# First two pairs of experts in TensorE's written order, and the branch for crowded experts moved behind the third pair's up products

## The chip, the cores and the metric

The kernel runs on one core of a Trainium2 chip. The metric is the time of one execution on the device, in microseconds (us), lower is better. A core has five engines that run side by side: TensorE (PE in the profile, with its weight loads as PEld), VectorE (DVE), ScalarE (ACT), GpSimd (POOL) and SyncE (SP). Here SP does no arithmetic: it issues the loads of all large weights. Engines wait for each other and for loads through semaphores.

## The reference, cut to what matters

Two blocks follow each other on 256 tokens of 1024 channels. The first has attention, a spatial gating unit and a mixture of experts; the second has convolutions, a linear recurrence and an MLP. The change lies in the mixture of experts, where every token goes to 2 of 32 experts:

```python
def hierarchical_moe(x, w_router_group, b_router_group, w_router_expert, b_router_expert,
                     w_gate, w_up, w_down):
    ...
    combine = (g_onehot[:, :, None] * (g_weight[:, None] * e_w)[:, None, :]).astype(x.dtype)
    out = jnp.zeros((n, D), dtype=x.dtype)
    for g in range(N_GROUPS):
        h = jax.nn.silu(jnp.einsum('nd,edf->nef', xt, w_gate[g])) * jnp.einsum('nd,edf->nef', xt, w_up[g])
        out = out + jnp.einsum('nef,efd->nd', h * combine[:, g, :, None], w_down[g])
    return out.reshape(B, S, D)
```

The kernel computes an expert only on the tokens that are routed to it, in 64 slots per expert.

## The kernel before, in words

**Pairs.** The 32 experts are taken as 16 pairs (`for i in range(16)`). A pair has 12 weight tiles of 1 MB (1,048,576 bytes) each: four of `w_gate`, four of `w_up`, four of `w_down`. For a pair, TensorE gathers the tokens of its slots into `xg` (L676, two halves of 16 matrix multiplies in the program, 32 passes in the trace for both), multiplies them with the gate tiles and the up tiles (L830), transposes the hidden activations `hs` into `hT` (L716), makes the slot tables of the next pair (`slots`, L692 and L697) and multiplies `hT` with the down tiles into `dn` (L964). ACT copies `dn` out as `y` (L722) and DVE makes its remainder (L723); later TensorE scatters `y` to the tokens (L729) and DVE adds it to `h` (L735). Between the up products and the transposes stands `act_mul`: ACT writes `silu(gate)` into `hs_hT` (L706) and DVE multiplies it with the up result (L707). DVE then copies the transposed tile (L717).

**Loads.** `Ring` holds the weight tiles in six pools (`ring_a` to `ring_f`, 5, 9, 2, 2, 1 and 2 buffers, 21 together). When a product has used up its tile, `ring.free` hands the buffer to the next tile in the list, and SP issues that load (L79) as soon as TensorE's last read of the buffer is over. SP issues in its own order, one load after the other. Each load counts on one of eight semaphores (`DMAHW0` to `DMAHW7`, in turn), and a load first waits for the one before it on the same semaphore, so at most eight are under way.

**Order.** From pair 2 on, `manual_schedule(engines={T.engine})` makes TensorE run in the order in which the code is written. For pairs 0 and 1 a scheduler orders TensorE's instructions.

**The branch.** An expert can have more than 64 tokens. `nmore` counts the blocks beyond; every engine reads it into a register `nb` (L943), and `overflow()` (branch at L841, loop at L868) works on these blocks if `nb > 0`. With the inputs of this case the loop isn't entered. In the loop SP loads weights into the buffer that `hidden()` gives, the same single buffer (tag `r4`) into which `hs_hT` and `y` of all pairs go:

```python
                w = hs_hT[:, 0].rearrange("p k c -> p (k c)")
...
                        nc.sync.dma_start(w, src[:, k // 2, k % 2])
```

In the kernel before, pair 1 ends with its whole scatter, and the branch stands between pair 1 and pair 2. After the last pair comes the second block, which begins with a normalisation of `h` and then multiplies with weights that come through `ring_a` alone (L1096).

Of the kernel before, what the change touches and what calls it, by code (L numbers as in the profile page):

```python
# [8 lines left out]
F32 = mybir.dt.float32  # L9
# [83 lines left out]
def kernel(ctx: ExitStack, tc: tile.TileContext, a: dict, out):  # L93
    nc = tc.nc
    V, S, T, G = nc.vector, nc.scalar, nc.tensor, nc.gpsimd
# [6 lines left out]
    ring = Ring(nc)  # L102
# [14 lines left out]
    W_EXP = []  # L117
# [50 lines left out]
    rows = p1m.tile([24, 128], F32, name="rows", tag="x41")  # L168
# [272 lines left out]
    ps = proj_ts(4)  # L441
# [290 lines left out]
    def scatter(gt, y, n, m):  # L732
        s = slice(512 * n, 512 * n + 512)
        for c in range(2):
            V.tensor_add(h[:, c, s], h[:, c, s], to_token(gt, c, m, y))  # L735

    def scatter_late(gt, y, dn, m):

        scatter(gt, y, 0, m)
        evac(dn, 1, m, y)  # L740
# [77 lines left out]
    nmore_i = mk.tile([128, 1], I32, name="nmore_i")  # L818
    V.tensor_copy(nmore_i, nmore)

    tile_done = []

    def products(i, n, ps, x, between=None):
        for q, idx in enumerate(W_EXP[i][n]):
            if q == 2 and between:
                between()
            t = ring.get(idx)
            for k in range(2):
                for j in range(2):
                    m = T.matmul(ps[64 * j:64 * j + 64, :], x[:, 2 * q + k, 64 * j:64 * j + 64], t[:, j, 512 * k:512 * k + 512],  # L830
                             start=q == 0 and k == 0, stop=q == 3 and k == 1, skip_group_check=True)
            ring.free(idx)
            if i == 0:
                tile_done.append(m)
                with tc.issue_after(m.ins):
                    for _ in range(2):
                        next(start, None)

    def overflow():

        with tc.If(nb > 0):  # L841
            nper = mk.tile([128, 32], F32, name="nper")
            V.tensor_add(nper, more[:, 0], more[:, 1])
            V.tensor_add(nper, nper, more[:, 2])
            pos = mk.tile([128, 3, 32], F32, name="pos")
            V.tensor_tensor_scan(pos[:, 0], ones[:, :32], nper, 0.0, op0=OP.mult, op1=OP.add)
            V.tensor_sub(pos[:, 0], pos[:, 0], nper)
            for m in (2, 1, 0):
                V.scalar_tensor_tensor(pos[:, m], pos[:, 0], float(m + 1), more[:, m], op0=OP.add, op1=OP.mult)
            V.tensor_scalar(pos, pos, -1.0, None, op0=OP.add)  # L850
            tabs = hidden()[:, 1].rearrange("p a (b c) -> p (a b) c", c=32).rearrange("p (m a) c -> p m a c", m=2)
            tab, sel = tabs[:, 0], tabs[:, 1]
            part = mk.tile([128, 8], F32, name="part")
            num = mk.tile([128, 32], F32, name="num")
            G.iota(num, pattern=[[1, 32]], base=0, channel_multiplier=0, allow_small_or_imprecise_dtypes=True)
            blocks = mk.tile([128, 2, 8], F32, name="blocks")
            V.memset(blocks, 0.0)
            for m in range(3):
                V.tensor_tensor(tab, iota[:, 0:8, None].to_broadcast([128, 8, 32]),
                                pos[:, m:m + 1, :].to_broadcast([128, 8, 32]), op=OP.is_equal)  # L860
                V.tensor_mul(sel, tab, num[:, None, :].to_broadcast([128, 8, 32]))
                V.tensor_reduce(part, sel, axis=AX.X, op=OP.add)
                V.tensor_add(blocks[:, 0], blocks[:, 0], part)
                V.tensor_reduce(part, tab, axis=AX.X, op=OP.add)
                V.scalar_tensor_tensor(blocks[:, 1], part, 64.0 * (m + 1), blocks[:, 1], op0=OP.mult, op1=OP.add)
            blocks_i = mk.tile([128, 8], I32, name="blocks_i")
            V.tensor_copy(blocks_i, blocks[:, 0])
            with tc.For_i(0, nb, 1) as b:  # L868
                ev = nc.sync.value_load(blocks_i[0:1, ds(b, 1)], min_val=0, max_val=31)
                evv = nc.vector.value_load(blocks_i[0:1, ds(b, 1)], min_val=0, max_val=31)  # L870
                cur = mw.tile([128, 7], F32, name="cur")
                V.tensor_copy(cur[:, 0:1], blocks[:, 1, ds(b, 1)])
                V.tensor_copy(cur[:, 1:3], rank[:, :, ds(evv, 1)].rearrange("t c o -> t (c o)"))
                V.tensor_scalar(cur[:, 1:3], cur[:, 1:3], cur[:, 0:1], None, op0=OP.subtract)
                V.tensor_copy(cur[:, 3:6:2], cwE[:, :, ds(evv, 1)].rearrange("t c o -> t (c o)"))
                V.tensor_copy(cur[:, 4:7:2], rf[:, :, 0])
                g = mw.tile([128, 2, 64], F32, name="g_ov", tag="onehot", bufs=1)
                V.tensor_tensor(g, iota[:, None, 1:65].to_broadcast([128, 2, 64]),
                                cur[:, 1:3, None].to_broadcast([128, 2, 64]), op=OP.is_equal)
                hs_hT = hidden()  # L880
                x = hs_hT[:, 1].rearrange("p a (b c) -> p (a b) c", c=64)
                for k0 in (0, 4):
                    gather_part(g, x, k0, 4)
                p = psM.tile([64, 2, 128], F32, name="ms")
                for c in range(2):
                    T.transpose(p[:, c], g[:, c], ident)
                gt = mk.tile([128, 2, 128], F32R, name="onehotT_ov")
                V.tensor_copy(gt[:64], p)
                p = psM.tile([64, 2], F32, name="ms")
                for c in range(2):  # L890
                    T.matmul(p, g[:, c], cur[:, 3 + 2 * c:5 + 2 * c], start=c == 0, stop=c == 1)
                cw = mk.tile([128, 2], F32, name="cw_ov")
                V.tensor_copy(cw[:64, 0:1], p[:, 1:2])
                V.tensor_mul(cw[:64, 1:2], p[:, 0:1], cw[:64, 0:1])
                ps = {}

                w = hs_hT[:, 0].rearrange("p k c -> p (k c)")
                for n in ("w_gate", "w_up"):
                    ps[n] = psE.tile([128, 512], F32, name="gate" if n == "w_gate" else "up")
                    src = flat[n][ds(ev, 1)].rearrange("o (q p k) f -> p (o q) k f", p=128, k=2)  # L900
                    for k in range(8):
                        nc.sync.dma_start(w, src[:, k // 2, k % 2])
                        T.matmul(ps[n][:64], x[:, k], w, start=k == 0, stop=k == 7)
                hT = transpose_h(act_mul(ps["w_gate"], ps["w_up"], cw, 64, hs_hT[:, 0]), 64, hs_hT[:, 1])
                dn = [psE.tile([128, 512], F32, name=f"dn{n}") for n in range(2)]
                src = flat["w_down"][ds(ev, 1)].rearrange("o (p k) f -> (o p) k f", k=4)
                for k in range(4):
                    for n in range(2):
                        nc.sync.dma_start(w, src[:, k, 512 * n:512 * n + 512])
                        T.matmul(dn[n][:64], hT[:, k, 0:64], w, start=k == 0, stop=k == 3)  # L910
                y = output()
                for n in range(2):
                    evac(dn, n, 64, y)
                    scatter(gt, y, n, 64)
# [8 lines left out]
    turn = ExitStack()  # L923
    steady = ExitStack()
    for i in range(16):
        if i == 2:


            steady.enter_context(tc.manual_schedule(engines={T.engine}))
        gate = psE.tile([128, 512], F32, name="gate")  # L930
        up = psE.tile([128, 512], F32, name="up")
        if i < 15:
            onehot(i + 1)
        products(i, "w_gate", gate, XG[i])
        if prev:
            scatter_late(*prev)
        if i == 0:
            with tc.issue_after(slots(0).ins):
                param_cols()
        with tc.issue_after(tile_done[0].ins) if i == 0 else ExitStack():  # L940
            products(i, "w_up", up, XG[i], (lambda: scatter(prev[0], prev[1], 1, 128)) if prev else None)
        if i == 0:
            nb = nc.values_load(nmore_i[0:1, 0:1], min_val=0, max_val=7)  # L943
        hs_hT = hidden()
        hs = act_mul(gate, up, CW[i], 128, hs_hT[:, 0])
        rows = gather(i + 1) if i < 15 else iter(())
        next(rows, None)
        if i < 2:
            next(rows, None)
            slots(i + 1)  # L950
        hT = transpose_h(hs, 128, hs_hT[:, 1])
        if 2 <= i < 15:
            next(rows, None)
            slots(i + 1)
        if i == 15:
# [14 lines left out]
        y = output()  # L970
        evac(dn, 0, 128, y)
        prev = (GT[i], y, dn, 128)
        if i == 1:
            scatter_late(*prev)
            scatter(GT[i], y, 1, 128)
            prev = None
            overflow()
    y2 = output("r2")
    evac(dn, 1, 128, y2)

# [537 lines left out]
```

## Time and profile before

| what | value |
|---|---|
| median of 3 runs (lowest to highest) | 1072.19 us (1071.92 to 1072.72) |
| the profiled execution's own time | 1072.1 us |
| its span, from the first to the last instruction | 1070.4 us |
| TensorE busy, share of the span | 1031.7 us, 96% |
| mean granted clock of TensorE | 0.985 of full speed |
| moved by DMA, mean rate | 299.70 MB, 280 GB/s |

The span is the time between the first and the last instruction of one profiled execution; 1.7 us of that execution's own time lie outside it. Busy shares are means over the whole span, and the stages have different limits, so the stretch from about 120 to 220 us, where the first three pairs run, is read by itself.

### The profile page before, as it was taken

To read this page: it belongs to the slowest core of one execution; us is meant where nothing else is said; L and a number is where in the kernel's file an instruction comes from. 1 tells how busy PE (TensorE), PEld (TensorE's weight loads), DVE (VectorE), ACT (ScalarE), POOL (GpSimd) and SP (SyncE) were. 2 spreads that over 40 slices of the span, in tenths; PEclk is the share of its full clock that TensorE was granted. 3 is DMA by queue.
4 is the path that set the end of the run, shared out by engine and by line. 5 is a ranking of instruction groups with operands and counts; after the bars stand their busy time and mean duration, and the time that the engine had idled before them with its cause. 6 is when DMAs were issued, how large, how long until landed. Compare 5 with 4: busy or idle time off the path is not lost.

```text
span 1070.4 us, 16246 instructions
## 1 busy us (share of the span) xinstructions
PE 1031.7 (96%) x6624; PEld 740.3 (69%) x6624; DVE 544.5 (51%) x1025; ACT 369.3 (34%) x596; POOL 221.4 (21%) x123
## 2 busy tenths in 40 slices
PE   8999998999999999999998899989897999999997
PEld 7998644444444444444444898869897999998996
DVE  4758433122222222222224889897986366555555
ACT  5565211000000000000002545866536445445443
POOL 0161000000000000000001887454885800000000
PEclk9999999999999999999999999989898999999999
DMA  9997899899999999999999664423462665655531
GB/s 315 301 358 278 311 368 410 339 409 409 408 409 410 409 409 409 409 408 409 409 409 368 190 196 160 133 88 117 158 197 95 193 206 185 205 181 180 195 117 40
DMA packets 138987, 299.70 MB, mean 280 GB/s; under 512 B 14325, under 2 KB 79325, under 8 KB 138909
## 3 DMA queue, kind: packets, MB, share of 16 engines
q1 hardware_dynamic: 138397, 297.32, 75.8%
q8 instruction: 53, 0.87, 0.3%
q10 hardware_dynamic: 432, 1.05, 0.2%
q0 software_dynamic: 80, 0.26, 0.1%
q14 instruction: 25, 0.20, 0.1%
HBM read 297.56 MB, written 1.05 MB: 279 GB/s over the span
## 4 chain that ended last, share of the span: by engine, by line
PE 72%; DVE 5%; issue 2%; POOL 1%; ACT 1%; POOLq 0%; DVEq 0%; ACTq 0%
PE acc L1096 22%; PE up L830 9%; PE dn L964 9%; PE gate L830 9%; PE acc L1416 8%; PE ms L676 5%; PE ms L729 3%; PE acc L1389 2%; PE acc L1347 2%; DVE acc L1158 1%; POOL w_lo L229 1%; PE acc L1224 1%; PE ms L716 1%; DVE vb L1247 1%; PE acc L1220 1%
## 5 line engine op out<-in xcount | busy, mean ns | idle before, releaser
L229 POOL TENSOR_TENSOR w_lo<-ring_a,w_hi 128x1024 fp32r<-128x1024 f32 (+1 forms) x77 | 186.4, 2437 | 535.3 <-ACT w_hi L228 534.4
L228 ACT ACTIVATE w_hi<-ring_a 128x1024 fp32r<-128x1024 f32 (+1 forms) x169 | 169.1, 1004 | 131.6 <-PE acc L1096 39.1
L229 DVE TENSOR_TENSOR w_lo<-ring_a,w_hi 128x1024 fp32r<-128x1024 f32 (+1 forms) x92 | 101.7, 1108 | 71.1 <-ACT w_hi L228 71.1
L1096 PE MATMUL acc<-n_hi,w_hi 128*128 128x256 f32 x448 | 119.3, 293 | 7.3 <-DVE rg L1236 4.6
L1096 PE MATMUL acc<-n_hi,w_lo 128*128 128x256 f32 x448 | 118.0, 290 | 1.8 <-POOL w_lo L229 1.8
L1158 DVE SCALAR_TENSOR_TENSOR acc<-ub,pcol,acc 128x256 f32<-128x256 f32 x232 | 104.0, 481 | 5.5 <-issue 2.8
L735 DVE TENSOR_TENSOR h<-h,ms 128x512 f32<-128x512 f32 x60 | 38.5, 683 | 125.7 <-PE ms L729 125.7
L722 ACT ACTIVATE y<-dn 128x512 fp32r<-128x512 f32 x32 | 19.0, 597 | 227.1 <-PE dn L964 113.0
L1096 PEld LDWEIGHTS acc<-n_hi,w_hi 128*128 128x128 f32 x448 | 88.2, 197 | 10.4 <-ACT acc L1229 4.7
L1096 PEld LDWEIGHTS acc<-n_hi,w_lo 128*128 128x128 f32 x448 | 88.1, 197 | 2.1 <-POOL w_lo L229 2.1
L723 DVE TENSOR_TENSOR y<-dn,y 128x512 fp32r<-128x512 f32 x32 | 21.9, 687 | 119.6 <-ACT y L722 119.6
L1096 PE MATMUL acc<-n_lo,w_hi 128*128 128x256 f32 x448 | 82.5, 286 | 0.0
L676 PEld LDWEIGHTS ms<-onehot,x_moe 128*128 128x128 f32 x512 | 59.9, 192 | 14.8 <-issue 13.0
L1096 PEld LDWEIGHTS acc<-n_lo,w_hi 128*128 128x128 f32 x448 | 66.9, 194 | 0.0
L676 PE MATMUL ms<-onehot,x_moe 128*128 128x128 f32 x512 | 64.4, 279 | 0.8 <-DVE onehot L666 0.8
L1096 PE MATMUL acc<-x2h,w_hi 128*128 128x256 f32 x256 | 64.6, 280 | 0.0
L1096 PE MATMUL acc<-x2h,w_lo 128*128 128x256 f32 x256 | 64.5, 281 | 0.0
L964 PE MATMUL dn<-ring_b,hs_hT 128*64 128x512 f32 x240 | 57.0, 597 | 0.0
L1416 PE MATMUL acc<-w_hi,fh 128*128 128x512 f32 x128 | 50.1, 391 | 0.0
L1416 PE MATMUL acc<-w_lo,fh 128*128 128x512 f32 x128 | 49.9, 390 | 0.0
L1416 PE MATMUL acc<-w_hi,fl 128*128 128x512 f32 x128 | 49.5, 391 | 0.0
L1096 PEld LDWEIGHTS acc<-x2h,w_hi 128*128 128x128 f32 x256 | 48.3, 189 | 0.6
(368 smaller groups left out, 2017.1 us busy)
## 6 DMA issues: line engine op xcount, KB each, us to landing
ring_a<-in_w_in_dram SPq DMA_DIRECT2D x32, 1024.0 KB, 9.1
ring_a<-in_w_dram SPq DMA_DIRECT2D x32, 1024.0 KB, 5.5
ring_b<-in_w_down_dram SPq DMA_DIRECT2D x30, 1024.0 KB, 18.4
ring_b<-in_w_gate_dram SPq DMA_DIRECT2D x26, 1024.0 KB, 18.3
ring_b<-in_w_up_dram SPq DMA_DIRECT2D x25, 1024.0 KB, 18.3
ring_a<-in_w_gate_dram SPq DMA_DIRECT2D x18, 1024.0 KB, 14.5
ring_a<-in_w_up_dram SPq DMA_DIRECT2D x15, 1024.0 KB, 12.1
ring_a<-in_w_down_dram SPq DMA_DIRECT2D x14, 1024.0 KB, 18.6
```

The costliest lines, as they stand in the source:

```text
L228: S.activation(hi[:, s], src[:, s], AF.Copy)
L229: steps.append(lambda s=s: E.tensor_sub(lo[:, s], src[:, s], hi[:, s].bitcast(F32)))
L676: T.matmul(p[:, k], xp[c][:, 128 * (k0 + k):128 * (k0 + k + 1)], g[:, c], start=c == 0, stop=c == 1)
L723: V.tensor_sub(y[:m, 1], dn[n][:m], y[:m, 0].bitcast(F32))
L729: T.matmul(p, gt[:m, c], y[:m, k], start=k == 0, stop=k == 1)
L735: V.tensor_add(h[:, c, s], h[:, c, s], to_token(gt, c, m, y))
L830: m = T.matmul(ps[64 * j:64 * j + 64, :], x[:, 2 * q + k, 64 * j:64 * j + 64], t[:, j, 512 * k:512 * k + 512], start=q == 0 and k == 0, st ...
L964: m = T.matmul(dn[n][64 * j:64 * j + 64], hT[:, k, 64 * j:64 * j + 64], t[:, j, 512 * n:512 * n + 512], start=k == 0, stop=k == 3, skip_gr ...
L1096: T.matmul(ps[:, b, :], w[:, k, b * 128:(b + 1) * 128], xx[4 * half + k], start=half == 0 and b == 0 and k == 0 and w is wh and not low, s ...
L1158: V.scalar_tensor_tensor(ca[:, j] if k == 30 else s, ub[:, j, k:k + 256], conv_a_w[:, 8 * k + j:8 * k + j + 1], s, op0=OP.mult, op1=OP.add)
L1347: T.matmul(pb[b // 2][:, b % 2, :], w[:, kk, b * 128:(b + 1) * 128], xx[:, kt], start=kt == 0 and b % 2 == 0 and q == 0, stop=kt == 11 and ...
L1416: T.matmul(out_ps[c][n], f[:, half, 128 * c:128 * c + 128], w[:, 0, 512 * n:512 * n + 512], start=j == 0 and half == 0 and q == 0, stop=j ...
```

## The change: what it does

Three things are done. First, TensorE's written order begins at pair 0. In pair 0 each gate tile is followed by the up tile of the same number, and the gathers that are still missing are written between them; pair 1 is written as all later pairs are, with pair 0's scatter inside its products. Second, `overflow()` moves from the end of pair 1 to a place in pair 2, behind its up products and ahead of its `act_mul`; pair 1's scatter goes into pair 2's products, and the one-hot table of pair 3 is made behind the branch. Third, since `gate`, `up` and `dn` are in use at the new place, the code in the branch takes its PSUM tiles from the pool `psM` (`ms`).

```diff
-    tile_done = []
-
-    def products(i, n, ps, x, between=None):
-        for q, idx in enumerate(W_EXP[i][n]):
-            if q == 2 and between:
-                between()
-            t = ring.get(idx)
-            for k in range(2):
-                for j in range(2):
-                    m = T.matmul(ps[64 * j:64 * j + 64, :], x[:, 2 * q + k, 64 * j:64 * j + 64], t[:, j, 512 * k:512 * k + 512],
-                             start=q == 0 and k == 0, stop=q == 3 and k == 1, skip_group_check=True)
-            ring.free(idx)
-            if i == 0:
-                tile_done.append(m)
-                with tc.issue_after(m.ins):
-                    for _ in range(2):
-                        next(start, None)
+    def product(i, n, ps, q):
+
+        t = ring.get(W_EXP[i][n][q])
+        for k in range(2):
+            for j in range(2):
+                T.matmul(ps[64 * j:64 * j + 64, :], XG[i][:, 2 * q + k, 64 * j:64 * j + 64], t[:, j, 512 * k:512 * k + 512],
+                         start=q == 0 and k == 0, stop=q == 3 and k == 1, skip_group_check=True)
+        ring.free(W_EXP[i][n][q])
...
-                    ps[n] = psE.tile([128, 512], F32, name="gate" if n == "w_gate" else "up")
+                    ps[n] = psM.tile([128, 512], F32, name="ms")
...
-                dn = [psE.tile([128, 512], F32, name=f"dn{n}") for n in range(2)]
+                dn = [psM.tile([128, 512], F32, name="ms") for n in range(2)]
...
     for i in range(16):
-        if i == 2:
-
-
+
+
+        if i == 0:
             steady.enter_context(tc.manual_schedule(engines={T.engine}))
         gate = psE.tile([128, 512], F32, name="gate")
         up = psE.tile([128, 512], F32, name="up")
-        if i < 15:
+        if i < 15 and i != 2:
             onehot(i + 1)
-        products(i, "w_gate", gate, XG[i])
-        if prev:
+        if i == 0:
+            for q in range(4):
+                for n, ps in (("w_gate", gate), ("w_up", up)):
+                    product(i, n, ps, q)
+                    for _ in range(2):
+                        next(start, None)
+                if q == 2:
+                    with tc.issue_after(slots(0).ins):
+                        param_cols()
+        else:
+            for q in range(4):
+                product(i, "w_gate", gate, q)
             scatter_late(*prev)
-        if i == 0:
-            with tc.issue_after(slots(0).ins):
-                param_cols()
-        with tc.issue_after(tile_done[0].ins) if i == 0 else ExitStack():
-            products(i, "w_up", up, XG[i], (lambda: scatter(prev[0], prev[1], 1, 128)) if prev else None)
+            for q in range(4):
+                if q == 2:
+                    scatter(prev[0], prev[1], 1, 128)
+                product(i, "w_up", up, q)
+        if i == 2:
+            steady.close()
+            overflow()
+            onehot(3)
+            steady.enter_context(tc.manual_schedule(engines={T.engine}))
...
-        if i < 2:
-            next(rows, None)
-            slots(i + 1)
         hT = transpose_h(hs, 128, hs_hT[:, 1])
-        if 2 <= i < 15:
+        if i < 15:
             next(rows, None)
             slots(i + 1)
...
-        if i == 1:
-            scatter_late(*prev)
-            scatter(GT[i], y, 1, 128)
-            prev = None
-            overflow()
```

How instructions move on the engines shows best at three places. The rows are the programs' orders, engine by engine; a row has the line, the operation, the tile written and the tiles read.

The first place is TensorE around the branch. In the kernel before, the last down products of pair 1 (`dn`), its scatter (`ms<-y,onehotT`), the register read and the branch stand together:

```order
L964 MATMUL dn_2047<-ring_a,hs_hT 64x512 x2
L964 MATMUL dn_2048<-ring_a,hs_hT 64x512 x2
L729 MATMUL ms<-y,onehotT 128x512 x8
L943 TENSOR_LOAD nmore_i
L841 COMPARE_AND_BRANCH
```

In the changed kernel, from pair 1's last down products to the branch (its line is now L832, that of the products L826), there stand:

```order
L966 MATMUL dn_2050<-ring_b,hs_hT 64x512 x2
L826 MATMUL gate<-ring_a,xg 64x512 x4
L826 MATMUL gate<-ring_b,xg 64x512 x4
L826 MATMUL gate<-ring_a,xg 64x512 x8
L729 MATMUL ms<-y,onehotT 128x512 x4
L826 MATMUL up<-ring_b,xg 64x512 x8
L729 MATMUL ms<-y,onehotT 128x512 x4
L826 MATMUL up<-ring_c,xg 64x512 x8
L832 COMPARE_AND_BRANCH
```

So the gate and up products of pair 2 have moved ahead of the branch, and the scatter now stands among them; the register read stands much earlier, behind pair 0's products.

The second place is SP, ahead of the branch. In the kernel before, the last of the 24 loads that stand between the read of `nmore_i` and the branch are these, with the semaphores that each waits for:

```order
L79 DMA ring_f<-in_w_up_dram 128x2x1024 [waits DMAHW6_49,PE_49]
L79 DMA ring_f<-in_w_up_dram 128x2x1024 [waits DMAHW7_49,PE_49]
L79 DMA ring_a<-in_w_up_dram 128x2x1024 [waits DMAHW0_49,PE_49]
L79 DMA ring_a<-in_w_up_dram 128x2x1024 [waits DMAHW1_49,PE_49]
L79 DMA ring_a<-in_w_down_dram 128x2x1024 [waits DMAHW2_49,PE_49]
L841 COMPARE_AND_BRANCH
L868 COMPARE_AND_BRANCH
L868 UNCONDITIONAL_BRANCH [waits SP_sequencer_49,DMAHW0_49,DMAHW1_49,DMAHW2_49,DMAHW3_49,DMAHW4_49,DMAHW5_49,DMAHW6_49,DMAHW7_49]
```

In the changed kernel there are 30 loads between the same two instructions, and the last of them are:

```order
L79 DMA ring_a<-in_w_down_dram 128x2x1024 [waits DMAHW3_49,PE_49]
L79 DMA ring_b<-in_w_down_dram 128x2x1024 [waits DMAHW4_49,PE_49]
L79 DMA ring_a<-in_w_down_dram 128x2x1024 [waits DMAHW5_49,PE_49]
L79 DMA ring_a<-in_w_gate_dram 128x2x1024 [waits DMAHW6_49,PE_49]
L79 DMA ring_b<-in_w_gate_dram 128x2x1024 [waits DMAHW7_49,PE_49]
L79 DMA ring_b<-in_w_gate_dram 128x2x1024 [waits DMAHW0_49,PE_49]
L832 COMPARE_AND_BRANCH
L859 COMPARE_AND_BRANCH
L859 UNCONDITIONAL_BRANCH [waits SP_sequencer_49,DMAHW0_49,DMAHW1_49,DMAHW2_49,DMAHW3_49,DMAHW4_49,DMAHW5_49,DMAHW6_49,DMAHW7_49]
```

Six more loads have moved ahead of the branch, and the last one now counts on `DMAHW0` instead of `DMAHW2`. The row with nine semaphores is the side on which the loop is skipped: SP waits there for all eight load semaphores.

The third place is ACT behind the branch. Before, from the end of the branch to the next pair's `hs_hT`:

```order
L841 UNCONDITIONAL_BRANCH [waits Activation_49]
L706 ACTIVATE hs_hT<-gate,cw 128x512 [waits DVE_49,DMAHW2_49,PE_49,Activation_49]
L694 ACTIVATE onehotT<-ms 128x256 [waits PE_49]
L722 ACTIVATE y<-dn_2378 128x512 [waits DVE_49,PE_49]
L722 ACTIVATE y<-dn_2379 128x512 [waits DVE_49,PE_49]
L706 ACTIVATE hs_hT<-gate,cw 128x512 [waits DVE_49,PE_49]
```

In the changed kernel:

```order
L832 UNCONDITIONAL_BRANCH [waits Activation_49]
L706 ACTIVATE hs_hT<-gate,cw 128x512 [waits DVE_49,DMAHW0_49,PE_49,Activation_49]
L694 ACTIVATE onehotT<-ms 128x256 [waits PE_49]
L722 ACTIVATE y<-dn_2381 128x512 [waits DVE_49,PE_49]
L722 ACTIVATE y<-dn_2382 128x512 [waits DVE_49,PE_49]
L706 ACTIVATE hs_hT<-gate,cw 128x512 [waits DVE_49,PE_49]
```

On ACT the rows read alike: in both kernels the first `hs_hT` behind the branch, that of pair 2, waits for one load semaphore, and the later ones for none. What moved is the branch ahead of it, and with it the load that this semaphore counts.

## Rows read from the trace of the kernel before

**Rows 1.** The page, parts 1 and 2: whole span, 40 slices of it.
```profile
span 1070.4 us, 16246 instructions
...
PE 1031.7 (96%) x6624; PEld 740.3 (69%) x6624; DVE 544.5 (51%) x1025; ACT 369.3 (34%) x596; POOL 221.4 (21%) x123
...
GB/s 315 301 358 278 311 368 410 339 409 409 408 409 410 409 409 409 409 408 409 409 409 368 190 196 160 133 88 117 158 197 95 193 206 185 205 181 180 195 117 40
```

**Rows 2.** The chain that ended last: start us, us, what; pair 2 on.
```profile
188.64 8.78 PE gate L830 x32
...
216.08 6.87 PE gate L830 x32
...
227.66 1.13 PE ms L729 x4
...
232.37 1.98 PE ms L676 x16
234.79 1.79 PE ms L676 x16
237.14 7.02 PE dn L964 x32
244.16 6.87 PE gate L830 x32
...
572.54 7.04 PE dn L964 x32
...
593.22 66.41 PE acc L1096 x552
```

**Rows 3.** TensorE's timeline, pairs 0 and 1: start us, us, line, tiles, idle before.
```profile
122.96 1.94 PE L830 MATMUL gate<-ring_a,xg 128*64 128x512 f32 x8
...
176.30 1.94 PE L964 MATMUL dn<-ring_f,hs_hT 128*64 128x512 f32 x8 [0.78 <-DVE hs_hT L717]
...
184.08 2.16 PE L729 MATMUL ms<-y,onehotT 128*128 128x512 f32 x6 [0.70 <-ACT y L722]
187.29 0.74 PE L729 MATMUL ms<-y,onehotT 128*128 128x512 f32 x2 [1.05 <-DVE y L723]
```

**Rows 4.** SP: two loads (timeline), and the branch's own instructions (source line).
```profile
183.43 0.37 SPq L79 DMA_DIRECT2D ring_a<-in_w_down_dram  x1
...
L841 SPq EVENT_SEMAPHORE  x9: 17/17/17, 184.4 to 194.4; - x9
...
194.53 0.38 SPq L79 DMA_DIRECT2D ring_a<-in_w_down_dram  x1
```

**Rows 5.** ACT's timeline behind the branch, and DVE's L707 (tile hs_hT).
```profile
197.51 0.69 ACT L706 ACTIVATE hs_hT<-gate,cw 128x512 f32<-128x512 f32 x1 [12.06 <-PE gate L830]
...
L707 DVE SCALAR_TENSOR_TENSOR hs_hT<-up,cw,hs_hT x16: 744/749/753, 141.3 to 569.3; 128x512 f32<-128x512 f32 x16
```

**Rows 6.** Windows: busy time of each engine, PEclk, DMA share, GB/s.
```profile
147.00:156.00 9.00, 9.00 (x46) 3.23 (x42) 0.05 (x1) 0.00 (x0) 0.00 (x0) 1.00 0.91 324
156.00:191.00 35.00, 31.50 (x149) 14.64 (x147) 11.07 (x20) 3.46 (x6) 0.00 (x0) 0.97 1.03 410
...
191.00:193.00 2.00, 2.00 (x10) 0.79 (x8) 0.00 (x0) 0.00 (x0) 0.00 (x0) 0.66 0.32 119
193.00:195.00 2.00, 2.00 (x12) 0.80 (x10) 0.00 (x0) 0.00 (x0) 0.00 (x0) 1.00 0.03 8
```

**Rows 7.** Windows at TensorE's lower clock, and TensorE's wait ahead of one.
```profile
189.00:192.30 3.30, 3.30 (x10) 1.22 (x8) 0.54 (x2) 0.00 (x0) 0.00 (x0) 0.50 0.79 312
...
708.90 0.55 PE L1096 MATMUL acc<-n_hi,w_hi 128*128 128x256 f32 x1 [4.56 <-DVE rg L1236]
...
707.80:714.50 6.70, 5.60 (x26) 5.64 (x27) 6.13 (x16) 6.67 (x14) 1.55 (x1) 0.50 0.00 0
```

**Rows 8.** The last loads of the experts: SP's timeline; the page's part 6.
```profile
552.85 9.67 SPq L79 DMA_DIRECT2D ring_a<-in_w_down_dram  x4
...
ring_b<-in_w_down_dram SPq DMA_DIRECT2D x30, 1024.0 KB, 18.4
```

## The prediction

> **What bounds the kernel now.** I first read the page's busy shares and slices [rows 1]: TensorE is busy for 1031.7 of 1070.4 us, and from the seventh slice to the 22nd DMA moves some 409 GB/s. So in the experts two things are near full at once, and the question is which of them ends last. The chain that ended last answers it for the time from 188 us on: it is TensorE alone, without a gap, from pair 2's gate at 188.64 to the last down products at 572.54, and a pair takes 244.16 - 216.08 = 28.08 us [rows 2]. Every microsecond by which pair 3's gate starts earlier or later than 216.08 therefore reaches the end of the experts. Behind them stand a normalisation and then, from 593.22, the second block's products, on the chain too [rows 2]; I take the shift through to the end unchanged.
>
> Ahead of 216.08, TensorE's own timeline shows where pairs 0 and 1 lose time [rows 3]: 0.78 us ahead of pair 1's down products, 0.70 and 1.05 us in pair 1's scatter, which has no other work beside it; the branch follows, and pair 2's gate takes 8.78 us where pair 3's takes 6.87 [rows 2], at a granted clock of 0.50, TensorE's 1.2 GHz level [rows 7].
>
> SP's timeline is what I looked at longest [rows 4]. Its last load ahead of the branch is issued at 183.43, the next one at 194.53. The nine waits of the branch lie between: SP waits until every load is in the core before it goes on. The windows agree [rows 6]: DMA runs at 410 GB/s up to 191, moves 119 in the next 2 us and 8 in the 2 after. This drain costs TensorE nothing now, since pair 2's gate and up tiles have long landed and its products run beside it. The first instruction behind the branch that needs the drain is ACT's L706 of pair 2, which writes the buffer that the skipped loop would have loaded into; its order row waits for the semaphore of the last load ahead of the branch. It started at 197.51, after 12.06 us in which it waited for TensorE's gate products [rows 5], 3 us after the drain's end. The wait was there, and something else ended later.
>
> **The change, part by part.**
>
> *Written order in pairs 0 and 1.* Pair 0 has 13.74 us of gate and up products (2 x 6.87 [rows 2]), three quarters of a gather (0.75 x (1.98 + 1.79) = 2.8) and one set of slots (237.14 - 234.79 - 1.79 = 0.56): 17.1 us from the first gate product at 122.96 [rows 3] makes 140.1. A gather, the transposes (234.79 - 232.37 - 1.98 = 0.44), slots and down products follow: 1.98 + 0.44 + 1.79 + 0.56 + 7.02 = 11.8, so pair 1's gate starts at about 151.9, and with the read of `nmore`, some half a microsecond, 152.4. Pair 1 takes 28.08 and pair 2 up to the end of its up products 232.37 - 216.08 = 16.29 [rows 2]: 196.8. If nothing else stood there, pair 3's gate would start 11.8 later, at some 209 with the branch, 7 us earlier than now. That is the most that this part can give on TensorE.
>
> *The branch behind pair 2's up products.* Now the drain stands right ahead of pair 2's L706, and there is no gate and up time of 16 us behind the branch to cover it. SP issues 30 loads ahead of the branch instead of 24. From 156 to 191 the loads ran at 410 GB/s without a hole [rows 6], so they are limited by transfer, not by free buffers; TensorE frees a buffer in 1.72 us (6.87 / 4) and a load takes 1.0486 MB / 410 GB/s = 2.56. Six more loads then end 6 x 2.56 = 15.4 us later: 194.53 + 15.4 = 209.9. One hole ahead may close: from 147 to 156 DMA moved 324 instead of 410 GB/s, which is 9 x (1 - 324 / 410) = 1.9 us, while SP waited for buffers that pair 0's down products now free one after the other; but their first comes no sooner than about 147, so I take half, 0.9, and as bounds 0 and 1.9. The drain ends at 209.0 (208.0 to 209.9).
>
> ACT then writes `hs` (0.69 us) [rows 5], DVE multiplies (0.75), TensorE transposes (0.44), gathers the second half (1.79), makes slots (0.56) and multiplies with the down tiles (7.02). The sum is 11.25, with 0.1 for the hand-overs 11.35: pair 3's gate at 209.0 + 11.35 = 220.35. The gather's first half needs no `hs` and is done by about 199.5, so TensorE stands for some 11 us.
>
> *The clock after that stand.* After a wait of 4.56 us the granted clock was 0.50 from about 707.8 to 714.5, and TensorE had begun again at 708.90 [rows 7], so 5.6 us of work ran at 1.2 GHz; of that half is lost, 2.8 us. The shorter stop ahead of pair 2's gate cost 8.78 - 6.87 = 1.91 us [rows 2]. This stand is longer than both; I take 2.6 and as bounds 1.0 (transposes and gather wait on ACT and DVE anyway, so a part may be hidden) and 3.2. Pair 3's gate starts at 222.95, which is 6.9 us later than 216.08.
>
> *What I cost at nothing.* All that is saved ahead of L706 (the stops of 0.78, 0.70 and 1.05 us, the slow gate of pair 2, up to 7 us in sum) is covered by the stand of 11 us. If that cover were gone, it would count in full. The early read of `nmore` and the one-hot of pair 3, now behind the branch, also end within the stand. The PSUM tiles in the loop concern instructions that don't run. The last down tile now lies in `ring_b`, so one more load of the second block may start early; from the last down products to 593.22 the chain waits on the normalisation, not on a load, so I count no gain.
>
> *The sum.* 6.9 us on the profiled execution's 1072.1 gives 1079.0. The median of the runs is 1072.19, 0.1 above that execution, so the two can be taken as one.
>
> The Trainium skill, on the page "DMA: Bandwidth & Descriptors" (section "Latency and other measured facts"), gives a fixed cost of about 2 us for a DMA, most of it the round trip of the receipt. The trace has more here: 238 KB moved from 191 on, 0.6 us' worth, so bytes ended at about 191.6 and SP went on 2.9 us later. By the page's figure the drain would end 0.9 us earlier and the time would be 1078.1; the measured tail is in the 194.53 that the sum starts from, so the sum keeps it.
>
> **The rivals.** *Faster: L706 doesn't stand behind the drain.* If the semaphore were met early, or if the loads landed before TensorE ends pair 2's up products at 196.8, TensorE's 7 us would come through. They would then meet the loads: the last down tiles are issued up to 562.5 and take 18.4 us from issue to landing [rows 8], while TensorE uses them from 572.54 to 579.58 [rows 2], so there are only some 3 us between, and 1 us from the closed hole. That gives about 4 us, 1068. For it: in the kernel before the same wait was invisible. Against it: it was invisible by 3 us only, and 15 us of loads are added. It decides where the drain ends: before 197 it is faster.
>
> *No change: the drain only moves.* If the drain lasted as long from its last load as now (194.53 - 183.43 = 11.1 us), that load would be issued when half of the up products are done, 232.37 - 227.66 = 4.7 us before their end, at 192.1, and the drain would end at 203.2; with 11.35 and 1.9 for the clock pair 3's gate starts at 216.5, 0.4 later: 1072.5. For it: nothing sets the queue's depth in the code but eight semaphores. Against it: TensorE would have freed 30 buffers in that time while DMA, at 2.56 us each and without a hole, cannot have moved more than some 24 or 25 of them.
>
> *Slower by more.* Loads could be held up further by SP's order, or the lower clock could fall into the down products for longer; each is inside the range.
>
> **How the numbers follow.** A measurement of this kernel tells 0.2%, 2.1 us, from no change. The forecast, a drain on the path, has a chance of 0.86; no change 0.06; faster 0.08. Its own bounds are 208.0 + 11.35 + 1.0 = 220.35 (4.3 later, 1076.4) and 209.9 + 11.35 + 3.2 = 224.45 (8.4 later, 1080.5). The stretches at the lower clock in the second block lie at other places after a shift and may add or take one loss of up to 1.7 us, so I give 1075.0 to 1082.0, and leave both rivals out.
>
> **What would show it.** Right: SP's first load behind the branch near 209; ACT's L706 of pair 2 right behind it, with its idle time ended by SP or a load and not by TensorE; a gap of 10 to 12 us on TensorE ahead of pair 2's transposes; a clock of 0.50 behind it; pair 3's gate near 223; 28.08 us a pair afterwards, and no gaps of a microsecond in pairs 0 and 1. Wrong would be the prediction if L706 started right after the up products, near 197; if SP's loads stopped well before 205; or if pairs behind the stand ran in less than 28 us, so that time was made good.

## The result, and the profile after

The changed kernel is slower: a median of 1079.43 us (1077.42 to 1080.12, 4 runs) against 1072.06 us for the kernel before on the same chip, a ratio of 1.0072 with a 95% interval of 1.0058 to 1.0086. The forecast was 1079.0, in a range of 1075.0 to 1082.0. The execution shown here took 1080.1 us, with a span of 1078.4; TensorE's busy time is 1033.8 us against 1031.7 [rows 1], so of the 8.0 us between the two spans 5.9 are time in which TensorE stood, and 2.1 are longer work.

TensorE's timeline of the changed kernel (start us, us, line, tiles, in brackets the idle time before and what ended it) shows where:

```profile
124.32 1.94 PE L826 MATMUL gate<-ring_a,xg 128*64 128x512 f32 x8
...
142.78 2.05 PE L676 MATMUL ms<-onehot,x_moe 128*128 128x128 f32 x16
...
154.47 3.60 PE L826 MATMUL gate<-ring_d,xg 128*64 128x512 f32 x16
...
182.54 1.89 PE L826 MATMUL gate<-ring_a,xg 128*64 128x512 f32 x8
...
195.34 3.65 PE L826 MATMUL up<-ring_c,xg 128*64 128x512 f32 x16
199.70 2.02 PE L676 MATMUL ms<-onehot,x_moe 128*128 128x128 f32 x16 [0.71 <-DVE onehot L666]
211.69 1.12 PE L716 MATMUL ms<-ident,hs_hT 128*128 128x128 f32 x4 [9.96 <-DVE hs_hT L707]
212.59 3.62 PE L676 MATMUL ms<-onehot,x_moe 128*128 128x128 f32 x16
```

The stops of [rows 3] are gone: no row of pairs 0 and 1 has a bracket. In their place stands one of 9.96 us in pair 2. The bracket names DVE's L707, which itself follows ACT's L706. ACT's timeline and SP's, of the same kernel, lead on:

```profile
210.16 0.69 ACT L706 ACTIVATE hs_hT<-gate,cw 128x512 f32<-128x512 f32 x1 [19.06 <-SPq L832]
```

```profile
192.61 2.08 SPq L79 DMA_DIRECT2D ring_b<-in_w_gate_dram  x2
210.67 0.38 SPq L79 DMA_DIRECT2D ring_c<-in_w_gate_dram  x1
```

In [rows 5] the idle time ahead of L706 was ended by TensorE's gate products; now the bracket names SP's branch, L832. What L706 itself waits for, by its order row, is `DMAHW0`, the semaphore of the last load ahead of the branch, and it starts 0.51 us before SP issues again: both follow the landing of that load. SP's two last loads ahead of the branch begin at 192.61 (the second at 194.3, by the row's length) and its next one stands at 210.67; before, the pair was 183.43 and 194.53 [rows 4]. The windows over this stretch (the last three columns are granted clock, DMA share and GB/s) show the loads running to their end, the empty time behind them, and the clock:

```profile
147.00:156.00 9.00, 9.00 (x47) 3.46 (x47) 2.01 (x7) 0.98 (x2) 0.00 (x0) 1.00 0.97 349
156.00:191.00 35.00, 35.00 (x178) 15.17 (x176) 7.71 (x16) 2.76 (x5) 0.00 (x0) 1.00 1.02 408
191.00:205.00 14.00, 10.02 (x52) 4.46 (x48) 2.87 (x5) 0.10 (x1) 0.00 (x0) 1.00 1.03 408
207.40:209.00 1.60, 0.00 (x0) 0.00 (x0) 0.00 (x0) 0.00 (x0) 0.00 (x0) 0.50 0.60 241
209.00:211.00 2.00, 0.00 (x0) 0.00 (x0) 0.12 (x1) 0.69 (x1) 0.00 (x0) 0.50 0.03 12
211.70:216.00 4.30, 4.30 (x20) 4.30 (x21) 1.22 (x2) 0.00 (x0) 0.00 (x0) 0.50 0.94 345
```

The chain that ended last shows that the delay is kept to the end:

```profile
224.31 6.87 PE gate L826 x32
...
252.38 6.87 PE gate L826 x32
...
580.77 7.04 PE dn L966 x32
...
601.53 67.67 PE acc L1093 x552
```

A pair still takes 252.38 - 224.31 = 28.07 us, the last down products start 8.23 us later than in [rows 2] and the second block 8.31 later. From there to the end of the span both kernels take 477 us.

### The profile page after: what moved, and what is told of

It is laid out like the page before. It is cut to its first block, busy times and chain, and to the rows that moved or that the text cites. A ratio compares the mean times of both kernels' runs of the same rounds, so it can differ in the third digit from the quotient of the medians.

```text
span 1078.4 us, 16243 instructions
## 1 busy us (share of the span) xinstructions
PE 1033.8 (96%) x6624; PEld 741.8 (69%) x6624; DVE 544.9 (51%) x1025; ACT 369.3 (34%) x596; POOL 222.2 (21%) x123
## 4 chain that ended last, share of the span: by engine, by line
PE 69%; DVE 5%; issue 2%; POOL 2%; ACT 2%; DMA 0%; POOLq 0%; DVEq 0%; ACTq 0%
PE acc L1093 21%; PE dn L966 9%; PE up L826 9%; PE gate L826 8%; PE acc L1413 8%; PE ms L676 5%; PE ms L729 3%; PE acc L1386 2%; PE acc L1344 2%; POOL w_lo L229 2%; DVE acc L1155 1%; PE ms L716 1%; DVE vb L1244 1%; DVE part L1294 0%; PE acc L1221 0%
## 5 line engine op out<-in xcount | busy, mean ns | idle before, releaser
L826 PE MATMUL up<-ring_b,xg 128*64 128x512 f32 x216 | 51.1, 597 | 0.0
```

The costliest lines, as they stand in the source:

```text
L826: T.matmul(ps[64 * j:64 * j + 64, :], XG[i][:, 2 * q + k, 64 * j:64 * j + 64], t[:, j, 512 * k:512 * k + 512], start=q == 0 and k == 0, st ...
```

## The experiments

All nine ran against the kernel before on the same chip as they did; the ratios are to that kernel. Its medians there were 1070.79 us for e1 to e4, 1071.96 for e5 to e9 and 1071.49 for e10, while the expectations start from 1072.1, or from 1079.4 for the changed kernel. So it is the ratios that are to be compared with them: e1's 1066.83 us is 0.9968 of its kernel before, 1068.7 on the scale of the expectations.

| run | what differs | median us | ratio, 95% interval |
|---|---|---|---|
| the change | | 1079.43 | 1.0072 (1.0058 to 1.0086) |
| e1_no_branch | changed kernel without the branch | 1066.83 | 0.9968 (0.9954 to 0.9982) |
| e2_own_buffer | changed kernel, the loop's loads into a buffer of their own | 1071.22 | 1.0004 (0.9995 to 1.0013) |
| e3_pool_loads | changed kernel, the loop's loads issued by POOL | 1067.38 | 0.9969 (0.9957 to 0.9981) |
| e4_order_only | written order, branch behind pair 1 | 1070.71 | 0.9998 (0.9989 to 1.0007) |
| e5_move_only | old order, branch in pair 2 | 1078.60 | 1.0067 (1.0050 to 1.0084) |
| e6_pair1 | changed kernel, branch in pair 1 | 1076.63 | 1.0051 (1.0032 to 1.0069) |
| e8_pair6 | changed kernel, branch in pair 6 | 1090.21 | 1.0180 (1.0163 to 1.0197) |
| e9_keep_busy | changed kernel, work in TensorE's stand | 1076.30 | 1.0041 (1.0027 to 1.0055) |
| e10_before_pool | kernel before, the loop's loads issued by POOL | 1070.82 | 0.9995 (0.9986 to 1.0004) |

**Take the branch away, or only its waits (e1 to e3).** Without the branch:

```diff
         if i == 2:
             steady.close()
-            overflow()
             onehot(3)
```

> The changed kernel without the branch and its loop (the blocks of experts with more than 64 tokens are left out; with these inputs none runs). Theory A, the drain on the path and behind it the pace of the loads: TensorE's stand of 10 us ahead of pair 2's transposes is gone, and with it the low clock; TensorE alone would then end the last down products 13.7 us earlier than in the changed kernel, 5.5 earlier than before. But from 192.2 us on, where the 59th load landed, the loads come at the 2.57 us that they took in the kernel before (128 of them from 216.14 to 545.29), so the 208th, the last down tile, lands near 575.3, and the last products end near 577.1 instead of 579.6: 1069.6 us, 2.5 under the kernel before. Rival B, TensorE alone bounds the experts: 1066.6. Rival C, the written order itself costs the time: it stays near 1079.

The loop's loads into a small buffer (`w_ov`, filled four times as often with a quarter each), so that nothing in `hs_hT`'s buffer is written by a load:

```diff
-                w = hs_hT[:, 0].rearrange("p k c -> p (k c)")
+                w = mk.tile([128, 128], F32, name="w_ov")
...
-                        nc.sync.dma_start(w, src[:, k // 2, k % 2])
+                        for f in range(0, 512, 128):
+                            nc.sync.dma_start(w, src[:, k // 2, k % 2, f:f + 128])
```

> The changed kernel, but the loop loads its weights into a small buffer of its own and not into the one that hs_hT uses, so ACT's L706 behind the branch waits for no load. SP's nine waits stay. Theory A: L706 of pair 2 starts right behind the up products, near 199; SP's loads still stop until about 210, the loads of 2.57 us each then end near 578.2 instead of 578.7 in the kernel before, and the end of the experts is where it was before: 1072.5 us, from 1071 to 1074. Rival B, TensorE alone bounds the experts: 1066.6. Rival C, the branch's own instructions or the empty load queue stop TensorE, whatever buffer is written: stays near 1079.

The same loads issued by POOL:

```diff
-                ev = nc.sync.value_load(blocks_i[0:1, ds(b, 1)], min_val=0, max_val=31)
+                ev = nc.gpsimd.value_load(blocks_i[0:1, ds(b, 1)], min_val=0, max_val=31)
...
-                        nc.sync.dma_start(w, src[:, k // 2, k % 2])
+                        nc.gpsimd.dma_start(w, src[:, k // 2, k % 2])
```

> The changed kernel, but the loop's loads are issued by POOL, so that the skipped side of the branch has no waits on SP's load semaphores. Theory A: no drain, no stop of SP's loads, no stand of TensorE, and the time is that of the kernel without the branch: 1069.6 us (last loads near 575.3). Rival B, TensorE alone: 1066.6. Rival C, the branch itself costs: near 1079; between 1070 and 1073 if compare and branch cost TensorE a microsecond or two.

ACT's row of L706 in pair 2, in the kernel with the buffer of its own and then in the one with POOL's loads:

```profile
200.25 0.69 ACT L706 ACTIVATE hs_hT<-gate,cw 128x512 f32<-128x512 f32 x1 [10.54 <-PEq L832]
```

```profile
197.87 0.69 ACT L706 ACTIVATE hs_hT<-gate,cw 128x512 f32<-128x512 f32 x1 [8.08 <-PEq L832]
```

And SP's timeline with the buffer of its own:

```profile
191.21 2.08 SPq L79 DMA_DIRECT2D ring_b<-in_w_gate_dram  x2
209.35 0.38 SPq L79 DMA_DIRECT2D ring_c<-in_w_gate_dram  x1
```

In e2 SP still stands from 193 to 209.35, and L706 starts at 200.25, nine microseconds before it is over and right behind TensorE's own branch (why that took until then is taken up in the last section). So it was the buffer that tied ACT, and through it TensorE, to the landing of SP's last load. A branch as such does not hold them, as e3 shows: the branch is in the same place, SP has no wait at it, and the time equals that of the kernel without it. Rival C, that the order or the branch itself costs, is out.

How much comes back was less clear beforehand. In e1 pair 3's gate starts at 209.53, 6.55 us earlier than in [rows 2], but the chain's end of the experts is a load, here cut from e1's chain:

```profile
555.71 17.26 DMA ring_b<-in_w_down_dram
572.97 0.04 issue
573.01 1.10 PE dn L965 x4
...
587.82 17.23 PE acc L1092 x134
```

The last down tile lands at 572.97, and TensorE has only four passes left to do then. With 363.5 us from pair 3's gate to the end of the experts, as in [rows 2], TensorE alone would have ended at 573.0; it ends at 574.1. So loads do set the end, as theory A says, but the limit lies 2.3 us earlier than I worked out (575.3): I had started from a landing in an execution whose experts began 1.3 us later than those of e1, and the 149 loads behind it came at 2.56 us and not at 2.57, which makes the rest. Measured in time, 0.32% or 3.4 us came back (0.18 to 0.46%), between A's 2.5 and B's 5.5 and nearer to A's.

**One half of the change at a time (e4, e5).** The order alone leaves the branch where it was, with pair 1's scatter ahead of it and the loop's old PSUM tiles:

```diff
         prev = (GT[i], y, dn, 128)
+        if i == 1:
+            scatter_late(*prev)
+            scatter(GT[i], y, 1, 128)
+            prev = None
+            steady.close()
+            overflow()
+            steady.enter_context(tc.manual_schedule(engines={T.engine}))
```

> Only the written order of pairs 0 and 1; the branch stands behind pair 1's whole scatter and the loop has its old PSUM tiles, as in the kernel before. Theory A: the drain ends near 194 and is covered by pair 2's gate and up products; TensorE would end the experts 1.3 to 3.2 us earlier, but the last loads land near 578.7 as before, so the time is 1071.5 to 1072.3, no change. Rival B, TensorE alone: 1069 to 1070.5. Rival C, the written order costs: over 1075.

The move alone takes the kernel before, and puts the branch into pair 2:

```diff
+        if i == 2:
+            steady.close()
+            overflow()
+            onehot(3)
+            steady.enter_context(tc.manual_schedule(engines={T.engine}))
         if i == 0:
             nb = nc.values_load(nmore_i[0:1, 0:1], min_val=0, max_val=7)
...
-        if i == 1:
-            scatter_late(*prev)
-            scatter(GT[i], y, 1, 128)
-            prev = None
-            overflow()
```

> Only the move: pairs 0 and 1 in the scheduler's order as in the kernel before, the branch behind pair 2's up products as in the changed kernel, the loop with the PSUM tiles of the changed kernel. Theory A, the drain sets the end of the stand: the same 30 loads stand ahead of the branch, they end some 0.5 to 1 us later than in the changed kernel since the hole ahead of 156 us stays, L706 of pair 2 starts at 210 to 211.5, and the time is that of the changed kernel or a little more, 1079.4 to 1081. Rival D, the move costs a fixed amount on TensorE and the written order gives 5 to 7 us back: 1084 to 1087.

ACT's L706 in pair 2 with the move alone:

```profile
209.69 0.69 ACT L706 ACTIVATE hs_hT<-gate,cw 128x512 f32<-128x512 f32 x1 [17.83 <-SPq L841]
```

The move alone costs what the whole change costs (1.0067 against 1.0072), and the order alone gives nothing that can be measured, though in e4 pair 3's gate starts at 213.62, 2.5 us before that of [rows 2]. Rival D is out: there is no cost of 12 us or more that a gain of 5 to 7 partly hides. L706 came 0.3 us earlier than the bounds I gave. Counted from the first gate product (122.90 in e5, 124.32 in the change), SP goes on after 87.30 us in e5 (210.20) and after 86.35 in the change, 0.95 us sooner with the written order. Part of that is the spread between executions: e9 below, whose loads up to this point are those of the change, has 210.05 - 123.17 = 86.88. Nothing else of the order reached the end.

**Move the branch (e6, e8).** The same lines at `i == 1` and at `i == 6`:

```diff
-        if i == 2:
+        if i == 6:
             steady.close()
             overflow()
-            onehot(3)
+            onehot(7)
```

> The changed kernel with the branch one pair earlier, behind pair 1's up products: 18 loads ahead of it instead of 30. Theory A: the 54th load lands 3 x 2.65 = 8 us behind the 51st (170.96 in the changed kernel), near 178.9; TensorE's up products of pair 1 end at 170.85, so the stand is 8.1 us instead of 11.3 and the time 3.2 less than that of the changed kernel: 1076.2 us, from 1075.5 to 1077.5. Rival E, a branch at this place of a pair costs the same in any pair: 1079.4.

> The changed kernel with the branch four pairs later, behind pair 6's up products: 78 loads ahead of it. Theory A: a pair takes TensorE 28.07 us and the loads 12 x 2.57 = 30.8, so the loads that are due fall behind by 2.8 a pair; the 114th lands at 210.7 + 48 x 2.57 = 334.1, the up products of pair 6 would end at 198.8 + 4 x 28.07 = 311.1. The stand is 23 us instead of 11.3: 1091 us, from 1089 to 1093. Rival E, a branch costs the same in any pair: 1079.4. Rival F, the drain is only the eight loads under way: their 8 x 2.57 = 20.6 us and 2.4 for what follows give at most 1089.

TensorE's rows of L716 behind the branch, in pair 1 and then in pair 6:

```profile
180.08 1.11 PE L716 MATMUL ms<-ident,hs_hT 128*128 128x128 f32 x4 [7.28 <-DVE hs_hT L707]
```

```profile
334.04 1.12 PE L716 MATMUL ms<-ident,hs_hT 128*128 128x128 f32 x4 [20.98 <-DVE hs_hT L707]
```

The stand is 7.28, 9.96 and 20.98 us in pairs 1, 2 and 6: 2.68 and 2.76 us for each pair that the branch goes later, where I had worked out 2.8 from the pace of the loads. The times follow. A branch is therefore not a fixed cost; it costs what the loads are behind TensorE at that moment. Rival F, that only the eight loads under way count, would have let L706 of pair 6 start at 310.3 (the end of the up products) + 8 x 2.57 = 330.9 at the latest; it starts at 332.51, since SP issued its last load ahead of the branch at 314.09 only. What counts is all loads that are due, also those that SP hasn't issued yet; F's 1089 and A's 1091 lie close together, though, and the time alone (1089.54 to 1092.31) would not have told them apart.

**Keep TensorE busy in the stand (e9).**

```diff
+        if i == 2:
+            busy = psM.tile([128, 4, 128], F32, name="ms")
+            for k in range(86):
+                T.transpose(busy[:, k % 4], ident, ident)
         hT = transpose_h(hs, 128, hs_hT[:, 1])
```

> The changed kernel with 86 transposes of the identity, some 9.5 us of work whose result is not used, on TensorE ahead of pair 2's transposes, where it stands for 10 us. Theory A: the drain ends as before, but the granted clock stays at 1.00, so that the gather's second half takes 1.8 us instead of 3.4 and the transposes 0.44 instead of 0.9: 2.6 us less than the changed kernel, 1076.8. If the low clock cost nothing on the path: 1079.4.

TensorE's timeline of this kernel around the stand:

```profile
198.56 2.02 PE L676 MATMUL ms<-onehot,x_moe 128*128 128x128 f32 x16 [0.71 <-DVE onehot L666]
200.42 9.55 PE L956 MATMUL ms<-ident 128*128 128x128 f32 x86
211.06 0.66 PE L716 MATMUL ms<-ident,hs_hT 128*128 128x128 f32 x4 [1.09 <-DVE hs_hT L707]
211.55 1.95 PE L676 MATMUL ms<-onehot,x_moe 128*128 128x128 f32 x16
```

and its windows from there on:

```profile
200.00:211.00 11.00, 9.97 (x92) 9.73 (x90) 0.75 (x2) 0.69 (x1) 0.00 (x0) 1.00 0.70 279
211.00:214.00 3.00, 2.94 (x27) 2.93 (x28) 1.75 (x4) 0.24 (x1) 0.00 (x0) 1.00 0.96 300
```

The granted clock is 1.00 throughout, the transposes take 0.66 us by their row instead of 1.12 and the gather's second half 1.95 instead of 3.62. From L706 to pair 3's gate it is 221.08 - 209.53 = 11.55 us here and 224.31 - 210.16 = 14.15 in the change: the lower clock cost 2.60 us, and the time fell by 0.3% of 1072 us, or 3.3.

**No drain in the kernel before (e10).** The edit of e3 in the kernel before.

> The kernel before with the one edit that POOL issues the loop's loads, so that SP passes the branch without a wait. Theory A: in the kernel before the drain was covered and TensorE's own order set pair 3's gate, so TensorE gains nothing; the loads run on and the last of them lands earlier, which nobody waits for: 1072 us, within 0.2% of the kernel before. Rival G: the pace of the loads alone set the end of the experts in the kernel before, and 3 us less of drain make it 1069.

SP passes its branch without a wait: its compare and branch stands at 184.3, among three loads that it issues from 183.84 to 193.1. The time is that of the kernel before. In this execution pair 2's gate took 7.09 us and not 8.78. If it did so in all executions of e10 and in none of the kernel before, the medians would differ by 1.69 us, or 0.16%; they differ by 0.05% (at most 0.14%), so the slow gate isn't shown to be a steady part of the time. Rival G is out: in the kernel before TensorE and not the loads set the end. With e4 and e3 the picture is complete: the better order alone gives nothing that can be measured, the missing drain alone neither (in the profiled executions the experts end at 578.0 in e4 and at 578.3 in e10, against 579.6 before, which the medians don't confirm), and both together give 0.31% (0.19 to 0.43). Each alone leaves the other limit standing: TensorE's own order in e10, and in e4 the loads, of which the last one that TensorE's up products of pair 15 wait for lands at 565.65 there and at 562.17 in e3. e3 is faster than both kernels and keeps the blocks for crowded experts; with these inputs no kernel here runs them.

## Why the prediction was right

*The branch's wait.* Right, and shown by e2: with another buffer L706 no longer waits for SP's last load.

*The drain's end.* Predicted at 209.0, SP goes on at 210.67. Of the 1.67 us, 1.36 were there before the experts began: the first gate product stands at 124.32 and not at 122.96. Counted from that product the drain ends after 86.35 us where 86.04 were worked out. The 0.9 us for half of a closed hole are not shown, though. The window of 147 to 156 has 349 GB/s instead of 324 [rows 6], but over the first 61.04 us behind the first gate product DMA moved 363 GB/s in the kernel before, in the change and in e5 alike, so the hole moved rather than closed. That e5 and the change differ by about as much, 0.95, is luck: without the term 86.9 would have been worked out, and e9 has 86.88.

*The drain's tail.* That the bytes ended at about 191.6 and SP went on 2.9 us later was misread. [rows 6] has 8 GB/s from 193 on, and smaller windows of the same trace show when nothing more moved:

```profile
192.50:193.50 1.00, 1.00 (x8) 0.48 (x6) 0.00 (x0) 0.00 (x0) 0.00 (x0) 1.00 0.11 33
193.50:194.50 1.00, 1.00 (x8) 0.39 (x6) 0.00 (x0) 0.00 (x0) 0.00 (x0) 1.00 0.00 0
```

The loads thinned out, and SP went on about 1 us behind the last bytes. The sum starts from 194.53 and is not touched by it.

*The products of pairs 0 and 1.* Pair 0 was mis-sized. From its first gate product to the end of its up products it took 142.78 - 124.32 = 18.5 us, not 17.1: the three quarters of a gather, in pieces of eight passes, took 1.09 us each, 3.3 instead of 2.8, and the changes between gathers and products took the rest. Pair 1 took 182.54 - 154.47 = 28.07, as forecast. The error of 1.4 us had no effect, since the drain ended behind it by 11.

*What follows L706.* 11.35 us at the full clock were forecast and e9 has 11.55; for the lower clock 2.6 were taken and 2.60 measured. These count from L706, and L706 starts 0.51 us before SP goes on, 85.84 us behind the first gate product, where the sum let it start at the drain's end, after 86.04. What follows it took 14.15 us where 13.95 were taken. Two errors of 0.20 us cancel.

*The sum.* From the first gate product to pair 3's gate the kernel before took 93.12 us and the changed one 99.99, a difference of 6.87, which is the 6.9 of the sum. The medians differ by 7.4 us. That it fits so closely is partly luck of the execution that was read: its 93.12 us hold the slow gate of pair 2, and e10's execution, without it, took 214.79 - 123.38 = 91.41, against which the change is 8.58 slower. The 1.7 us by which the range was widened, for stretches at the lower clock in the second block, are shown by no run; from that block's first products to the end of the span it is 477.2 us before and 476.9 in the change.

*Costed at nothing.* The early reads and the one-hot of pair 3 made a stop of 0.71 us ahead of the gather, inside the time in which TensorE would have stood anyway. The load of the second block that may start earlier gave nothing: that block's products start 8.31 us later, which is the delay of the experts.

*The rivals.* The faster one named its point of decision, the drain's end before 197, and e3 is that case: there the gain met the loads, as forecast. That it was 3.3 us where I had written 4 is partly luck, since 3 of the 4 were slack between the loads and TensorE that the rows don't give: a tile issued by 562.5 and 18.4 us on its way [rows 8] lands at 580.9, behind its last use at 579.58. In e4, with the drain left in place, a pair 3 that starts 2.5 us earlier gave at most 0.11%. What e3 gains is that the loads themselves run earlier. SP's last two down tiles there:

```profile
553.96 4.87 SPq L79 DMA_DIRECT2D ring_b<-in_w_down_dram  x2
```

They are issued by 558.83, and in the kernel before by 552.85 + 9.67 = 562.52 [rows 8].

No change by a drain that only moves would have needed an end at 203.2. Counted from the first gate product the end moved by 86.35 - (194.53 - 122.96) = 14.78 us, near the 15.4 of the six loads that were added.

## What to carry to other kernels

A branch that isn't taken can still empty a load queue, if the queue's engine has loads inside it, and a buffer that such a load would write then ties later writers to that emptying. Ask of such a branch how far the loads are behind at its place, and how much work stands between it and the first instruction that touches that buffer; if the loads can go through a queue that is idle, the question falls away. Where two engines are near full, a gain on one shows only when the other has been given room too.

## What was not expected of the hardware

TensorE's compare and branch took 0.36 us in the changed kernel and 0.45 in the one before, but 6.08 us in e2, by the row of the source view of e2:

```profile
L832 PEldq COMPARE_BRANCH  x1: 6082/6082/6082, 194.0 to 194.0; - x1
```

TensorE stood for 3.17 us behind it, and pair 3's gate came at 214.23 where e3, without that, has 210.22. The loop that is skipped is longer in e2, since each of its loads and products is cut in four. The Trainium skill says on the page "Runtime: NRT & Kernel Launch" (section "Instruction fetch mechanics") that a taken branch to a place outside the instructions already fetched has to wait until a DMA has brought them. That fits: DMA was moving 406 GB/s at the time, and only e2 has the longer loop. But no run here changed the length of the loop alone, so the cause stays open. There remains the question which of the two, this stop or the drain of the loads, kept e2 at the time of the kernel before. From e2's chain:

```profile
547.69 18.30 DMA ring_f<-in_w_up_dram
...
566.03 1.96 PE up L826 x8
...
571.34 7.04 PE dn L968 x32
```

With 363.5 us from pair 3's gate to the end of the experts, as in [rows 2], TensorE would have ended them at 577.7, the stop included; it waited for an up tile that landed at 565.99, and ended at 578.38. So in this execution the loads set the end, and the stop was covered.

In the change TensorE's granted clock, at 2.4 GHz while it worked, was 0.50 (1.2 GHz) in the windows from 207.40 on, when it stood, and in the window from 211.70 to 216.00, when it worked again; so the stand cost some time twice, and e9 got the second part back with work that nobody needs.
